# Expert selection of a two-block model: gates of all heads normalised in one go, and a triangle of 112 candidate sums in place of a 16 x 16 square

## The chip, the cores and the metric

One core of a Trainium2 chip runs the whole program once. The metric is the device time of one execution in microseconds (us). The kernel before takes 2967.11 us (median of three runs, 2965.75 to 2971.43).

The engines are named as the profile names them: PE is TensorE (PEld its weight loads), DVE is VectorE, ACT is ScalarE, POOL is GpSimd and SP is SyncE. Each engine works through its own instructions in the order in which the program issues them; between engines they wait on semaphores.

## The reference, cut to what matters

Two transformer blocks over 256 tokens of width 2048. The change is in the second block's mixture of experts (PEER): for each token and each of eight heads, two lists of 128 key scores are cut to their sixteen largest, all sums of one key of either list are formed, the sixteen largest sums choose sixteen experts, and a softmax over these sixteen sums gives the gates.

```python
v1, i1 = lax.top_k(s1, PEER_TOPK)
v2, i2 = lax.top_k(s2, PEER_TOPK)
cand = (v1[..., :, None] + v2[..., None, :]).reshape(B, S, PEER_HEADS, PEER_TOPK * PEER_TOPK)
vs, ci = lax.top_k(cand, PEER_TOPK)
e1 = jnp.take_along_axis(i1, ci // PEER_TOPK, axis=-1)
e2 = jnp.take_along_axis(i2, ci % PEER_TOPK, axis=-1)
eidx = e1 * PEER_NKEYS + e2
gates = jax.nn.softmax(vs, axis=-1).astype(xn.dtype)
...
act = jax.nn.gelu(jnp.einsum('tkd,td->tk', expert_u[ib], xb))
return jnp.einsum('tk,tkd->td', act * gb, expert_v[ib])
```

So every token has 8 x 16 = 128 experts, and each of these needs a row of `expert_u` (2048 floats) for its activation and a row of `expert_v` for its output.

## The kernel before

The 256 tokens stand as two tiles of 128 partitions (`tt` is 0 or 1). The part in question runs like this.

**Scores.** `project1` makes the 16 query blocks on PE from weight chunks that SP loads (`raw<-w_pq`). `pq_done` copies a block from PSUM on ACT, `score` multiplies it by the keys on PE and writes the scaled scores to `sc` on ACT. Head h has its scores when two such blocks are through.

**Choice.** `topk(0)` works through heads 0, 2, 4, 6 and `topk(1)` through 1, 3, 5, 7; both are Python generators in lanes that are stepped in turn after every second matmul of the projection (`beside`). So the order on each engine is fixed when the program is written. For one head:

- `top16` on the four lists of 128 scores, on DVE: the eight largest, their positions, removal of these eight, the next eight, their positions;
- on POOL the positions are cast (L1599) and two squares of 16 x 16 sums are formed (L1601);
- `top16` on DVE on the two lists of 256 sums; `vs` are the values and `ci` the positions;
- the decode on POOL (L1606 to L1611): the position is cast to float, divided by 16 and rounded by adding and subtracting a large constant, which gives the row; 16 times the row is taken off, which gives the column. L1612 negates the largest sum;
- a comparison on DVE (L1616) of these numbers with 0 to 15, four multiplications on POOL by the keys' positions (L1618), a sum on DVE (L1624), and three instructions on POOL that form the expert's number and put it in `idx` (L1626 to L1628);
- for the gates an exponential with its sum on ACT (L1620, two instructions), a reciprocal on DVE (L1625) and a scaling on POOL (L1633).

**Rows.** As soon as a head has its `idx`, `u_rows` lets POOL issue gathers (L1663): one gather brings one row of `expert_u` for each of 128 tokens, into one of ten seats (four for the second tile of tokens). DVE multiplies each by the tokens (L1703, 256 times) and sums it, which frees the seat for the gather ten further on. While the heads are still being chosen, these multiplications stand between the steps of `topk` on DVE.

**After the eighth head** `slots_` copies the gates (L1640) and transposes the experts' numbers (L1644 to L1647). When 128 multiplications of a tile of tokens are done, `weights` applies the activation and the gates. `spots` then builds matrices for the dense half of `expert_v`, which PE multiplies at L1900, and the other half is gathered and summed by `v_rows` (L1840).

Of the kernel before, what the change touches and what calls it, by code (L numbers as in the profile page):

```python
# [10 lines left out]
U32 = mybir.dt.uint32  # L11
AF = mybir.ActivationFunctionType
OP = mybir.AluOpType
AX = mybir.AxisListType

T = 256
# [209 lines left out]
def program(tc, A, out, stage=99, dbg=None):  # L226
# [26 lines left out]
    V, S, G, PE, SP = nc.vector, nc.scalar, nc.gpsimd, nc.tensor, nc.sync  # L253
# [333 lines left out]
    p = bank(bgN, "pn")  # L587
# [47 lines left out]
    bias = cM(8, T)  # L635
# [4 lines left out]
    wide = cM(2, 128)  # L640
# [14 lines left out]
    oh, past = cW(512, p=32), cW(512, p=8)  # L655
# [872 lines left out]
    xs = dram.tile([128, 16, T], F32, name="xs")  # L1528
    SP.dma_start(xs, x)
    cK = Carve("cK")  # L1530
    subk, qring, eg, ek, kk = cK(8, 2, 128), cK(4, T), cK(2, 128), cK(8, 2, 2, 16), cK(2, 128)
    G.dma_start(subk.rearrange("p h s n -> p (h s n)"), A["subk"])
    sc = slab("sc").rearrange("p (t h s n) -> p t h s n", t=2, h=8, s=2)
    cT = Carve("cT")
    e1T, e2T, wT = sq[:, 0], sq[:, 1], acc_sq
    gate_ = rb.rearrange("p (t s) -> p t s", t=2)
    wv = sm.rearrange("p a b -> p (a b)").rearrange("p (t s) -> p t s", t=2)
# [47 lines left out]

    def topk(first):

        cand, oh = cT(2, 16, 16), cT(2, 2, 16, 16)
        vv, ii, iif = cT(2, 2, 16), cT(2, 2, 16).bitcast(U32), cT(2, 2, 16)
        vs, ci, cf, c1, gs = cT(2, 16), cT(2, 16).bitcast(U32), cT(2, 16), cT(2, 2, 16), cT(2, 4)  # L1590
        xf = cT(2, 16)
        flat = lambda v: v.rearrange("p t s n -> p (t s n)")
        for h in range(first, 8, 2):
            while flags.get(("sc", h), 0) < 2:
                yield
            hs = slice(h * 16, h * 16 + 16)
            both = [(tt, s) for tt in range(2) for s in range(2)]
            yield from top16([(sc[:, tt, h, s], vv[:, tt, s], ii[:, tt, s]) for tt, s in both])
            G.tensor_copy(iif, ii)  # L1599
            for tt in range(2):  # L1600
                G.tensor_add(cand[:, tt], vv[:, tt, 0][:, :, None].to_broadcast([128, 16, 16]),  # L1601
                             vv[:, tt, 1][:, None, :].to_broadcast([128, 16, 16]))
            yield
            yield from top16([(cand[:, tt].rearrange("p a b -> p (a b)"), vs[:, tt], ci[:, tt]) for tt in range(2)])

            G.tensor_copy(cf, ci)  # L1606
            G.tensor_scalar(c1[:, :, 0], cf, 1.0 / 16, -7.5 / 16, op0=OP.mult, op1=OP.add)
            G.tensor_scalar(c1[:, :, 0], c1[:, :, 0], 1.5 * 2.0 ** 23, None, op0=OP.add)
            G.tensor_scalar(c1[:, :, 0], c1[:, :, 0], 1.5 * 2.0 ** 23, None, op0=OP.subtract)
            G.tensor_scalar(c1[:, :, 1], c1[:, :, 0], -16.0, None, op0=OP.mult)  # L1610
            G.tensor_add(c1[:, :, 1], c1[:, :, 1], cf)  # L1611
            G.tensor_scalar(gs[:, :, 0], vs[:, :, 0], -1.0, None, op0=OP.mult)  # L1612
            io = iota[:, 0:16][:, None, :].to_broadcast([128, 64, 16])
            yield
            sel = oh.rearrange("p t s a b -> p (t s a) b")
            V.tensor_tensor(sel, flat(c1)[:, :, None].to_broadcast([128, 64, 16]), io, op=OP.is_equal)  # L1616
            for tt, s in both:
                G.tensor_mul(oh[:, tt, s], oh[:, tt, s], iif[:, tt, s][:, None, :].to_broadcast([128, 16, 16]))  # L1618
            for tt in range(2):
                S.activation(eg[:, tt, hs], vs[:, tt], AF.Exp, bias=gs[:, tt, 0:1], accum_out=gs[:, tt, 1:2])  # L1620
            yield
            yield
            yield
            V.tensor_reduce(flat(ek[:, h]), sel, axis=AX.X, op=OP.add)  # L1624
            V.reciprocal(gs[:, :, 2], gs[:, :, 1])  # L1625
            G.tensor_scalar(xf, ek[:, h, :, 0], 128.0, None, op0=OP.mult)  # L1626
            G.tensor_add(xf, xf, ek[:, h, :, 1])
            G.tensor_copy(idx[:, :, hs], xf)  # L1628
            flags[("idx", h)] = True
            yield  # L1630
            for tt in range(2):
                g = eg[:, tt, hs]
                G.tensor_scalar(g, g, gs[:, tt, 2:3], None, op0=OP.mult)  # L1633
            flags["heads"] = flags.get("heads", 0) + 1

    def slots_():

        while flags.get("heads", 0) < 8:
            yield
        G.tensor_copy(gate_, eg)  # L1640
        for tt in range(2):
            p = bank(bgA, "pa")
            for k in range(2):
                G.tensor_copy(kk[:, k].rearrange("p (h n) -> p h n", h=8), ek[:, :, tt, k])  # L1644
                PE.transpose(p[:, k * 128:k * 128 + 128], kk[:, k], ident)
            for k, d in enumerate((e1T, e2T)):
                S.copy(d[:, tt * 128:tt * 128 + 128], p[:, k * 128:k * 128 + 128])  # L1647
            yield
        flags["topk"] = True
# [228 lines left out]
    for k in range(128):  # L1878
# [14 lines left out]
        for j in range(8):  # L1893
            w, _ = next_block()
# [60 lines left out]
```

## Time and profile before

| what | value |
|---|---|
| median of three runs | 2967.11 us |
| the profiled execution's own time | 2963.08 us |
| its span, first to last instruction | 2961.3 us |
| busy: PE, DVE, ACT, POOL | 2311.8, 1999.7, 1191.2, 900.9 us |
| mean granted clock of TensorE | 0.878 of full speed |
| groups of instructions at L1703: count, busy | 256, 580.3 us |

The shares over the whole span say little here, since the program runs in stages with different limits. The choice of experts lies between about 1519 and 1702 us of the span, the stream of `expert_u` rows between 1542 and about 2270 us, the dense half of `expert_v` and the second stream of rows behind that. To read the profile, one goes to that stretch: what the chain of work that ended last runs through there, and whether the DMA engines are full.

### The profile page before, as it was taken

What the parts mean: (1) busy time and instruction counts of PE and PEld (TensorE: products, weight loads), DVE (VectorE), ACT (ScalarE), POOL (GpSimd) and SP (SyncE); (2) the same over time, 40 slices, a digit from 0 to 9 for tenths busy, and PEclk for the clock granted to TensorE, in tenths of its full rate; (3) what the DMA queues carried; (4) which work ended last, traced back from release to release, by engine and by line L of the source; (5) the groups of instructions that cost most, each with busy time, mean ns of one, the idle gap of its engine ahead of it and who ended that gap; (6) DMA issues with size and microseconds to landing.
All of it is one profiled execution on the core that took longest, in us unless ns stands there. A gap on an engine that the chain in (4) does not pass through costs nothing.

```text
span 2961.3 us, 39499 instructions
## 1 busy us (share of the span) xinstructions
PE 2311.8 (78%) x14635; PEld 2106.1 (71%) x14635; DVE 1999.7 (68%) x2615; ACT 1191.2 (40%) x2560; POOL 900.9 (30%) x1262
## 2 busy tenths in 40 slices
PE   8999999999999999999997200022222999999799
PEld 8887898888889999998986200011122988888689
DVE  5455666555556565656537999988998866666655
ACT  4355555444444454445411000058880444400043
POOL 3202215111111000331135543333334555555420
PEclk9999999999999999999998655555555799999999
DMA  6444455655655555543557799999997799999945
GB/s 221 153 128 122 134 158 180 196 188 187 197 187 190 185 180 184 172 151 109 182 201 279 291 407 422 422 397 408 415 415 317 265 403 404 395 401 409 366 148 166
DMA packets 174675, 765.11 MB, mean 258 GB/s; under 512 B 19585, under 2 KB 22049, under 8 KB 141201
## 3 DMA queue, kind: packets, MB, share of 16 engines
q1 hardware_dynamic: 99216, 353.83, 36.0%
q0 software_dynamic: 75264, 408.75, 34.5%
q8 instruction: 115, 1.88, 0.3%
q14 instruction: 80, 0.65, 0.1%
HBM read 757.77 MB, written 4.21 MB: 257 GB/s over the span
## 4 chain that ended last, share of the span: by engine, by line
PE 59%; DMA 12%; DVE 10%; issue 9%; POOL 8%; ACT 1%; another core or an unknown queue 0%; SPq 0%; POOLq 0%; DVEq 0%; ACTq 0%
PE acc L411 11%; PE acc L1900 7%; PE acc L386 6%; PE acc L388 6%; PE acc L387 6%; DMA rows<-w_vs,idx 6%; PE acc L412 6%; POOL rows L1663 5%; DMA rows<-w_u,idx 5%; DVE rows L1703 5%; PE acc L485 3%; PE acc L483 3%; PE acc L484 3%; PE sp L1794 1%; DMA raw<-w_vd 1%
## 5 line engine op out<-in xcount | busy, mean ns | idle before, releaser
L350 DVE TENSOR_TENSOR wlo<-raw,whi 128x1024 fp32r<-128x1024 f32 (+1 forms) x501 | 613.5, 1233 | 415.1 <-ACT whi L349 408.3
L349 ACT CAST whi<-raw 128x1024 fp32r<-128x1024 f32 (+1 forms) x501 | 519.7, 1042 | 380.2 <-PE acc L387 130.9
L1703 DVE SCALAR_TENSOR_TENSOR rows<-rows,yt 128x2048 f32<-128x2048 f32 x256 | 580.3, 2285 | 42.9 <-DMA rows<-w_u,idx 38.6
L1900 PE MATMUL acc<-G,raw 128*128 128x256 f32 x2048 | 457.3, 385 | 12.4 <-DMA raw<-w_vd 11.1
L1900 PEld LDWEIGHTS acc<-G,raw 128*128 128x128 f32 x2048 | 391.8, 193 | 71.7 <-DMA raw<-w_vd 17.0
L1840 DVE SCALAR_TENSOR_TENSOR sacc<-rows,sm,sacc 128x1024 f32<-128x1024 f32 x254 | 327.3, 1289 | 143.8 <-DMA rows<-w_vs,idx 127.4
L1663 POOL DMA_INDIRECT rows<-w_u,idx x256 | 244.2, 954 | 380.0 <-DVE rows L1703 274.8
L1663 POOL DMA_INDIRECT rows<-w_vs,idx x256 | 248.8, 972 | 149.6 <-DVE sacc L1840 81.7
L411 PE MATMUL acc<-xl,whi 128*128 128x512 f32 x704 | 248.2, 391 | 0.0
L411 PE MATMUL acc<-xh,whi 128*128 128x512 f32 x704 | 248.1, 391 | 0.0
L1762 PE MATMUL sp<-P,Q 128*128 128x128 f32 x256 | 60.2, 430 | 213.9 <-ACT P L1758 213.9
L1762 PEld LDWEIGHTS sp<-P,Q 128*128 128x128 f32 x256 | 55.8, 330 | 218.6 <-ACT P L1758 218.6
L564 POOL TENSOR_TENSOR acc_sq<-acc_sq,sq 128x256 f32<-128x256 f32 x63 | 57.0, 904 | 504.6 <-ACT sq L563 502.7
L485 PE MATMUL acc<-ring,wlo 128*128 128x256 f32 x704 | 199.3, 283 | 0.1
L483 PE MATMUL acc<-ring,whi 128*128 128x256 f32 x704 | 199.3, 283 | 0.1
L484 PE MATMUL acc<-ring,whi 128*128 128x256 f32 x704 | 199.2, 283 | 0.0
L412 PE MATMUL acc<-xh,wlo 128*128 128x256 f32 x704 | 197.2, 280 | 0.0
L412 PE MATMUL acc<-xl,wlo 128*128 128x256 f32 x704 | 197.1, 280 | 0.0
L1659 PE MATMUL yt<-keep,xg 128*128 128x128 f32 x32 | 5.6, 350 | 237.6 <-DVE rows L1703 237.1
L1191 POOL TENSOR_TENSOR hT<-cF 128x256 f32<-128x256 f32 x44 | 70.8, 1609 | 372.7 <-ACT whi L349 342.8
L1659 PEld LDWEIGHTS yt<-keep,xg 128*128 128x128 f32 x32 | 5.0, 184 | 238.1 <-DVE rows L1703 237.3
L386 PE MATMUL acc<-xh,whi 128*128 128x256 f32 x520 | 150.6, 290 | 3.2 <-ACT whi L349 1.8
(486 smaller groups left out, 5692.7 us busy)
## 6 DMA issues: line engine op xcount, KB each, us to landing
raw<-w_gu SPq DMA_DIRECT2D x176, 512.0 KB
raw<-w_vd SPq DMA_DIRECT2D x128, 512.0 KB
raw<-w_down SPq DMA_DIRECT2D x88, 512.0 KB
raw<-w_out SPq DMA_DIRECT2D x32, 512.0 KB
raw<-w_pq SPq DMA_DIRECT2D x32, 512.0 KB
raw<-w_pg SPq DMA_DIRECT2D x32, 512.0 KB
raw<-w_b SPq DMA_DIRECT2D x24, 512.0 KB
raw<-w_lat SPq DMA_DIRECT2D x18, 512.0 KB
```

Of the source, the lines that this page charges most:

```text
L349: S.copy(hi[j][:, a:b], raw[j][:, a:b])
L350: V.tensor_sub(lo[j][:, a:b], raw[j][:, a:b], hi[j][:, a:b].bitcast(F32))
L386: PE.matmul(ps, wh, xh, start=start, stop=False, **k)
L411: PE.matmul(ps, wh, xh.both(k), start=k == 0, stop=False, skip_group_check=True)
L412: PE.matmul(ps[:, :T], wl, xh[:, k], start=False, stop=k == kb - 1, skip_group_check=True)
L483: PE.matmul(o, wh, ah, start=(k == 0 and j % 2 == 0), stop=False, skip_group_check=True)
L484: PE.matmul(o, wh, al, start=False, stop=False, skip_group_check=True)
L485: PE.matmul(o, wl, ah, start=False, stop=(k == nk - 1), skip_group_check=True)
L1663: G.indirect_dma_start(dst, None, src, bass.IndirectOffsetOnAxis(ap=idx[:, tt, s:s + 1], axis=0))
L1703: V.scalar_tensor_tensor(r, r, 1.0, accT, op0=OP.mult, op1=OP.mult, accum_out=wv[:, tt, s:s + 1])
L1840: V.scalar_tensor_tensor(sacc, r, w, sacc, op0=OP.mult, op1=OP.add)
L1900: PE.matmul(o, w, gs_[k // 16][:, k % 16], start=(k == 0 and j % 2 == 0), stop=k == 127, skip_group_check=True)
```

## The change

The two squares of 256 sums become two lists of 112: rows 0 to 3 of the square with all 16 columns (64 sums) and rows 4 to 15 with columns 0 to 3 (48 sums). The position in such a list no longer is 16 times the row plus the column, so the decode has more steps. The sixteen largest sums of every head go to one tile `vsa`, and the exponential, its sum, the reciprocal and the scaling are made once for all heads, in `slots_`.

```diff
-        cand, oh = cT(2, 16, 16), cT(2, 2, 16, 16)
+        cand, oh = cT(2, 112), cT(2, 2, 16, 16)
...
             for tt in range(2):
-                G.tensor_add(cand[:, tt], vv[:, tt, 0][:, :, None].to_broadcast([128, 16, 16]),
-                             vv[:, tt, 1][:, None, :].to_broadcast([128, 16, 16]))
-            yield
-            yield from top16([(cand[:, tt].rearrange("p a b -> p (a b)"), vs[:, tt], ci[:, tt]) for tt in range(2)])
+                for a, na, nb, at in ((0, 4, 16, 0), (4, 12, 4, 64)):
+                    G.tensor_add(cand[:, tt, at:at + na * nb].rearrange("p (a b) -> p a b", a=na),
+                                 vv[:, tt, 0, a:a + na][:, :, None].to_broadcast([128, na, nb]),
+                                 vv[:, tt, 1, 0:nb][:, None, :].to_broadcast([128, na, nb]))
+            yield
+            vs = vsa[:, h]
+            yield from top16([(cand[:, tt], vs[:, tt], ci[:, tt]) for tt in range(2)])
 
             G.tensor_copy(cf, ci)
-            G.tensor_scalar(c1[:, :, 0], cf, 1.0 / 16, -7.5 / 16, op0=OP.mult, op1=OP.add)
-            G.tensor_scalar(c1[:, :, 0], c1[:, :, 0], 1.5 * 2.0 ** 23, None, op0=OP.add)
-            G.tensor_scalar(c1[:, :, 0], c1[:, :, 0], 1.5 * 2.0 ** 23, None, op0=OP.subtract)
-            G.tensor_scalar(c1[:, :, 1], c1[:, :, 0], -16.0, None, op0=OP.mult)
-            G.tensor_add(c1[:, :, 1], c1[:, :, 1], cf)
-            G.tensor_scalar(gs[:, :, 0], vs[:, :, 0], -1.0, None, op0=OP.mult)
+            i_, j_, r_ = c1[:, :, 0], c1[:, :, 1], 1.5 * 2.0 ** 23
+            G.tensor_scalar(i_, cf, 1.0 / 16, -7.5 / 16, op0=OP.mult, op1=OP.add)
+            G.tensor_scalar(i_, i_, r_, None, op0=OP.add)
+            G.tensor_scalar(i_, i_, r_, None, op0=OP.subtract)
+            G.tensor_scalar(j_, cf, 0.25, -12.375, op0=OP.mult, op1=OP.add)
+            G.tensor_scalar(j_, j_, r_, None, op0=OP.add)
+            G.tensor_scalar(j_, j_, r_, None, op0=OP.subtract)
+            G.tensor_scalar(far, cf, 1.0 / 112, -7.5 / 112, op0=OP.mult, op1=OP.add)
+            G.tensor_scalar(far, far, r_, None, op0=OP.add)
+            G.tensor_scalar(far, far, r_, None, op0=OP.subtract)
+            G.tensor_sub(j_, j_, i_)
+            G.tensor_mul(j_, j_, far)
+            G.tensor_add(i_, i_, j_)
+            G.tensor_scalar(xf, i_, 12.0, -48.0, op0=OP.mult, op1=OP.add)
+            G.tensor_mul(xf, xf, far)
+            G.tensor_scalar(j_, i_, -16.0, None, op0=OP.mult)
+            G.tensor_add(j_, j_, cf)
+            G.tensor_add(j_, j_, xf)
...
-            for tt in range(2):
-                S.activation(eg[:, tt, hs], vs[:, tt], AF.Exp, bias=gs[:, tt, 0:1], accum_out=gs[:, tt, 1:2])
...
-            V.reciprocal(gs[:, :, 2], gs[:, :, 1])
...
-            for tt in range(2):
-                g = eg[:, tt, hs]
-                G.tensor_scalar(g, g, gs[:, tt, 2:3], None, op0=OP.mult)
...
     def slots_():
 
         while flags.get("heads", 0) < 8:
             yield
-        G.tensor_copy(gate_, eg)
+        for _ in range(2):
+            yield
+        wide = [128, 16, 16]
+        gs = kk.rearrange("p k n -> p (k n)")[:, 0:16]
+        G.tensor_copy(gs, ga[:, :, 0])
+        G.tensor_tensor(ga, ga, gs[:, :, None].to_broadcast(wide), op=OP.subtract)
+        yield
+        S.activation(ga, ga, AF.Exp)
+        for _ in range(2):
+            yield
+        V.tensor_reduce(gs, ga, axis=AX.X, op=OP.add)
+        V.reciprocal(gs, gs)
+        G.tensor_mul(gate_.rearrange("p t (h n) -> p h t n", h=8), vsa, gs.rearrange("p (h t) -> p h t", t=2)[:, :, :, None]
+                     .to_broadcast([128, 8, 2, 16]))
```

The order of the instructions on PE and SP is the same in both kernels, and on DVE and ACT it differs by the instructions named above alone. On POOL, the decode of one head stands like this before (`cT` is the slab that holds all small tiles of `topk`; a wait on Pool_49 is a wait for an earlier instruction of POOL itself):

```order
L1606 CAST cT<-cT 128x32 [waits DVE_49]
L1607 TENSOR_SCALAR cT<-cT 128x2x16 [waits Pool_49]
L1608 TENSOR_SCALAR cT<-cT 128x2x16 [waits Pool_49]
L1609 TENSOR_SCALAR cT<-cT 128x2x16 [waits Pool_49]
L1610 TENSOR_SCALAR cT<-cT 128x2x16 [waits Pool_49]
L1611 TENSOR_TENSOR cT<-cT 128x2x16 [waits Pool_49]
L1612 TENSOR_SCALAR cT<-cT 128x2
L1618 TENSOR_TENSOR cT<-cT 128x256 [waits DVE_49]
```

In the changed kernel the same place begins like this on POOL:

```order
L1612 CAST cT<-cT 128x32 [waits DVE_49]
L1614 TENSOR_SCALAR cT<-cT 128x2x16 [waits Pool_49]
L1615 TENSOR_SCALAR cT<-cT 128x2x16 [waits Pool_49]
L1616 TENSOR_SCALAR cT<-cT 128x2x16 [waits Pool_49]
L1617 TENSOR_SCALAR cT<-cT 128x2x16
L1618 TENSOR_SCALAR cT<-cT 128x2x16 [waits Pool_49]
L1619 TENSOR_SCALAR cT<-cT 128x2x16 [waits Pool_49]
L1620 TENSOR_SCALAR cT<-cT 128x32
L1621 TENSOR_SCALAR cT<-cT 128x32 [waits Pool_49]
L1622 TENSOR_SCALAR cT<-cT 128x32 [waits Pool_49]
L1623 TENSOR_TENSOR cT<-cT 128x2x16
L1624 TENSOR_TENSOR cT<-cT 128x2x16 [waits Pool_49]
```

Six more follow (L1625 to L1630, all but L1628 with a wait on Pool_49) before the multiplications, which are L1636 there. The comparison on DVE (L1616 before, L1634 in the changed kernel) waited for the sixth of these instructions and now waits for the eighteenth.

Behind the eighth head POOL's order was this (`rows` are the seats, `cK` holds the gates and the experts' numbers, `rb` takes the gates):

```order
L1628 CAST idx<-cT 128x2x16 [waits Pool_49]
L1633 TENSOR_SCALAR cK<-cK,cT 128x16 [waits DVE_49]
L1633 TENSOR_SCALAR cK<-cK,cT 128x16 [waits Activation_49]
L1640 COPY rb<-cK 128x256 [waits Pool_49]
L1644 COPY cK<-cK 128x128 x2
L1663 DMA rows_15108<-w_u,idx 128x2048 [waits DMASW6_49,DVE_49]
L1644 COPY cK<-cK 128x128 [waits PE_49] x2
L1663 DMA rows_15109<-w_u,idx 128x2048 [waits DMASW7_49,DVE_49]
```

In the changed kernel POOL has there:

```order
L1643 CAST idx<-cT 128x2x16 [waits Pool_49]
L1688 DMA rows_15108<-w_u,idx 128x2048 [waits DMASW6_49,DVE_49]
L1688 DMA rows_15109<-w_u,idx 128x2048 [waits DMASW7_49,DVE_49]
L1656 COPY cK<-cT 128x16
L1657 TENSOR_TENSOR cT<-cT,cK 128x256 [waits Pool_49]
L1688 DMA rows_15109<-w_u,idx 128x2048 [waits DMASW0_49,DVE_49]
L1688 DMA rows_15110<-w_u,idx 128x2048 [waits DMASW1_49,DVE_49]
L1688 DMA rows_15110<-w_u,idx 128x2048 [waits DMASW2_49,DVE_49]
L1664 TENSOR_TENSOR rb<-cT,cK 128x8x2x16 [waits DVE_49,Activation_49]
L1669 COPY cK<-cK 128x128 [waits Pool_49]
L1669 COPY cK<-cK 128x128
L1688 DMA rows_15106<-w_u,idx 128x2048 [waits DMASW3_49]
```

Five gathers now stand ahead of the gates' last step (L1664), which waits for DVE's reciprocal; the sixth gather stands behind it.

## Rows read from the trace of the kernel before

**Rows 1.** Busy time of each engine in stretches: start:end, length, then each engine.
```profile
core 0: us, PE busy (x) PEld busy (x) DVE busy (x) ACT busy (x) POOL busy (x), PEclk, DMA share, GB/s
1600.00:1690.00 90.00, 37.48 (x155) 31.52 (x153) 82.29 (x219) 6.72 (x27) 43.58 (x80) 0.71 0.81 308
1690.00:1702.00 12.00, 0.00 (x0) 0.00 (x0) 10.47 (x23) 0.69 (x4) 8.21 (x14) 0.50 0.54 190
1702.00:1790.00 88.00, 1.42 (x4) 0.73 (x4) 88.00 (x81) 2.15 (x5) 39.53 (x49) 0.50 0.99 407
1790.00:1930.00 140.00, 0.00 (x0) 0.00 (x0) 130.82 (x117) 0.00 (x0) 52.45 (x56) 0.50 1.01 422
1930.00:2250.00 320.00, 64.11 (x273) 59.26 (x273) 287.66 (x251) 238.81 (x770) 115.97 (x125) 0.55 1.00 410
```
**Rows 2.** Chain that ended last, head 2: start us, us, what.
```profile
1568.72 0.81 DVE cT L1583 x2
1569.59 0.22 POOL cT L1606
1569.89 0.23 POOL cT L1607
1570.20 0.31 POOL cT L1608
...
1570.96 0.30 POOL cT L1610
1571.34 0.26 POOL cT L1611
1571.62 1.24 DVE cT L1616
1572.93 2.79 POOL cT L1618 x4
1575.74 1.22 DVE cK L1624
```
**Rows 3.** The same chain at heads 0, 1 and 5.
```profile
1540.67 0.09 DVE cT L1625
...
1543.41 0.65 POOL cK L1633 x2
...
1550.67 0.95 POOL rows L1663
1551.62 0.23 POOL cT L1606
...
1644.23 0.20 POOL cT L1612
```
**Rows 4.** Groups of 1490 to 1790 us: busy us, mean ns | idle before.
```profile
L1601 POOL TENSOR_TENSOR cT<-cT 128x256 f32<-128x256 f32 x16 | 9.6, 618 | 0.0
...
L1580 DVE MAX8 cT<-sc 128x8 f32<-128x128 f32 x32 | 6.9, 277 | 0.0
...
L1580 DVE MAX8 cT<-cT 128x8 f32<-128x256 f32 x16 | 5.9, 413 | 0.0
```
**Rows 5.** Waits, 1490 to 1800 us: total us, times, longest us.
```profile
ACT cK L1620 <- POOL cT L1612: 109.9, 8, 21.0
...
DVE cT L1572 <- ACT sc L1555: 18.4, 2, 14.9
...
DVE cT L1616 <- POOL cT L1611: 13.5, 5, 4.8
```
**Rows 6.** Instructions of DVE and POOL around the end of the eighth head, in time.
```profile
1644.27 1.22 DVE L1616 TENSOR_TENSOR cT<-cT,keep 128x1024 f32<-128x1024 f32 x1
...
1700.81 1.22 DVE L1624 TENSOR_REDUCE cK<-cT 128x64 f32<-128x1024 f32 x1 [1.52 <-POOL cT L1618]
...
1702.02 2.27 DVE L1703 SCALAR_TENSOR_TENSOR rows<-rows,yt 128x2048 f32<-128x2048 f32 x1
...
1704.21 2.28 DVE L1703 SCALAR_TENSOR_TENSOR rows<-rows,yt 128x2048 f32<-128x2048 f32 x1
```

More of the change, by code (lines that the diff above doesn't have):

```diff
@@ L1530, in program @@
     cK = Carve("cK")
-    subk, qring, eg, ek, kk = cK(8, 2, 128), cK(4, T), cK(2, 128), cK(8, 2, 2, 16), cK(2, 128)
+    subk, qring, ek, kk = cK(8, 2, 128), cK(4, T), cK(8, 2, 2, 16), cK(2, 128)
     G.dma_start(subk.rearrange("p h s n -> p (h s n)"), A["subk"])
@@ L1534, in program @@
     cT = Carve("cT")
+    vsa = cT(8, 2, 16)
+    ga = vsa.rearrange("p h t n -> p (h t) n")
     e1T, e2T, wT = sq[:, 0], sq[:, 1], acc_sq
@@ L1586, in topk @@
     def topk(first):
-        cand, oh = cT(2, 16, 16), cT(2, 2, 16, 16)
+        cand, oh = cT(2, 112), cT(2, 2, 16, 16)
         vv, ii, iif = cT(2, 2, 16), cT(2, 2, 16).bitcast(U32), cT(2, 2, 16)
-        vs, ci, cf, c1, gs = cT(2, 16), cT(2, 16).bitcast(U32), cT(2, 16), cT(2, 2, 16), cT(2, 4)
-        xf = cT(2, 16)
+        ci, cf, c1 = cT(2, 16).bitcast(U32), cT(2, 16), cT(2, 2, 16)
+        xf, far = cT(2, 16), cT(2, 16)
         flat = lambda v: v.rearrange("p t s n -> p (t s n)")
```

## The prediction

> **What bounds the kernel now.** The shares over the whole span do not help, so I read three things for the stretch of the change. First the busy time by stretch [rows 1]. From 1702 us on, the DMA engines are full (share 0.99 to 1.01, 405 to 422 GB/s) until the rows of `expert_u` have come, at about 2250. Ahead of that they are not: 0.81 in 1600 to 1690, and 0.54 in the last 12 us before the eighth head is done. Ahead of 1702 DVE is what is busy (82.29 of 90 us), with holes. So the row stream becomes a fixed amount of transfer that starts at full rate only when the choice of experts ends, and the end of the choice (the sum over head 7's comparison, L1624 at 1700.81 [rows 6]) is what carries the rest of the program with it.
>
> Second, the chain of waits in that stretch [rows 2]. For head 2 it leaves DVE after the last position search (L1583), goes through every small POOL instruction of the decode (1569.59 to 1571.60, 2.01 us), back to DVE for the comparison (1571.62), to POOL for the multiplications (2.79 us) and to DVE for the sum. The decode is on the path, instruction by instruction. Third, the waits [rows 5]: DVE stood 13.5 us for the decode in five of eight heads, while scores made it wait 18.4 us in only two places, both ahead of the first head. ACT waited 109.9 us for the decode, but nobody on the path waited for ACT.
>
> **The change part by part.**
>
> **Shorter lists on DVE.** Per head ten instructions (four MAX, four index searches, two replacements) run over 112 columns and not 256. A MAX takes 277 ns over 128 columns and 413 over 256 [rows 4], so 136 ns go per 128 columns, which I take for the searches and replacements too: 0.136 x 144 / 128 = 0.153 us per instruction. Nine of ten count: between the two first MAX DVE waits for POOL's sums, which come no sooner. That is 9 x 0.153 = 1.38 us per head. In head 1 it gives nothing: POOL is busy with five gathers until 1551.62 and starts the decode right behind them, later than DVE is ready [rows 3]. So 7 x 1.38 = 9.6 us go.
>
> **Sums on POOL.** Two adds of 256 columns at 618 ns [rows 4] become four of 64 or 48. A POOL instruction of two inputs takes 0.25 us for 32 columns (L1611 [rows 2]), so a column costs (0.618 - 0.25) / 224 = 0.0016 us, and the new ones 0.30 and 0.28: 0.58 for a list against 0.62. Nothing.
>
> **The decode.** Before, the comparison waited for six instructions, 2.01 us; it now waits for eighteen. Their spacing comes from [rows 2]. The cast is followed after 0.30 us. A scaling with two operations (L1607) is followed by an instruction that needs its result after 0.31 us. One with a single operation (L1608) is followed by such an instruction after 0.38 us, of which it is busy 0.30; where the next one needs nothing of it I take these 0.30. An instruction with two inputs is busy 0.25; with the same gap of 0.08 it is followed after 0.33. Of the eighteen: one cast (0.30), four scalings with two operations (L1614, L1617, L1620, L1626: 1.24), four single ones followed by a dependent one (L1615, L1618, L1621, L1628: 1.52), three followed by an independent one (L1616, L1619, L1622: 0.90), four of two inputs followed by a dependent one (1.32), one not (0.25), and the last (0.26). The sum is 5.79 us, 3.78 more than before, and 8 x 3.78 = 30.2 us over eight heads. Is any of it hidden? Where nothing stands between search and comparison on DVE (heads 0 to 3) it is bare. In heads 5 to 7 one row multiplication stands between (2.2 us), but the old decode filled that cover already: in head 5 the last instruction of the decode ends at 1644.23, where L1612 starts [rows 3], and the comparison starts at 1644.27 [rows 6]. So all of it is on the path.
>
> Bounds from both sides: if each of the twelve added instructions took the shortest spacing that these rows show for any, 0.22 us, the decode grows by 2.6 us (21.1 in all); if the longest, 0.38, by 4.6 (36.5). I take 3.78, since the order tells which depend on the one before, and since the rows are of the same shape.
>
> The Trainium skill speaks against this term: its page "GPSIMD Engine Reference", section "Instruction dispatch", puts the cost of a POOL instruction's dispatch at tens of cycles, and its section "Elementwise — side-by-side cycle accounting" the elements at about 2.6 cycles each. By that page a 32-column instruction is, as my estimate at the 1.2 GHz that "Trainium Kernel Development and Optimization" gives, about 0.1 us, twelve are 1.2 us, and the change would come out near no change. The trace does not agree: the same shape holds POOL 0.22 to 0.31 us.
>
> **What leaves the path with the gates.** The reciprocal leaves DVE: 0.09 us per head [rows 3], 0.7 in all. The two scalings L1633 stood ahead of the next head's sums in head 1 only (0.65 us [rows 3]); elsewhere POOL waited for DVE there. L1612 (0.20 [rows 3]) stood between decode and multiplications where a gather follows it, heads 1, 5 and 7: 0.6. ACT loses sixteen exponentials, so PE's scores and the last weight chunks come sooner; I put that at nothing, because DVE never waited for scores after the first head [rows 5], and no transfer leaves the full stretch by it (DMA is idle for 46% of the 12 us before 1702 [rows 1], so those chunks are through).
>
> **The gates behind the last head.** POOL's last step of the gates waits for DVE's reciprocal, which stands behind six row multiplications, and the sixth gather is queued behind it. That gather waits for the sixth of these multiplications anyway, so what is added is the sum over 256 columns and the reciprocal on DVE and three POOL instructions, some 1.5 to 2 us. The next gathers catch up, since a gather holds POOL for 0.95 us [rows 3] and seats come free every 2.2 us (L1703 starts at 1702.02 and 1704.21 [rows 6]). By then five gathers have been issued faster than they land, 2.2 against 1.05 MB / 422 GB/s = 2.49 us [rows 1], so the DMA engines have work meanwhile. I put it at nothing, 2 us if that cover fails. The gates are needed only when 128 rows are done, after 1930.
>
> **Sum.** 30.2 - 9.6 - 0.7 - 0.65 - 0.6 = 18.7 us later at the end of the eighth head. Behind it the stream is transfer at a full rate and everything else hangs on it, so the end moves by as much: the profiled execution's 2963.08 becomes 2981.8. The median of the runs stands 4.0 above that execution, so I predict 2967.1 + 18.7 = 2985.8 us. With the two bounds of the decode the sum is 9.6 and 25.0: 2977 to 2992.
>
> **The rivals.**
>
> *Faster: a long train of small POOL instructions costs only its columns.* If the fixed part of each vanished behind the one before, an added instruction would cost 32 x 0.0016 = 0.05 us, twelve 0.6, eight heads 4.9, and 4.9 - 11.5 = -6.6 us gives 2960.5. It decides from 11.5 / 96 = 0.12 us per added instruction down. For it: the dependent ones are spaced by a wait, and five of the added have none. Against it: the old train of six takes 2.01 us, 0.33 each. By the page named above the price lies near this point. Chance 0.06.
>
> *The same: the stream of rows swallows it.* The rows' transfers are a fixed amount, and were gathers queued deep enough at 1702, a later end of the choice would only eat into the queue. It takes 18.7 / 2.49 = 7.5 gathers in the queue. For it: the DMA engines are full for all of the next 550 us. Against it: 0.54 in the last 12 us. The time would be about 2967. Chance 0.10.
>
> *More: the spacing is longer, and the gates hold the stream up.* All twelve at 0.38 us and above, the wait for the reciprocal not covered: 25.0 + 2 and more, 2994 to 2997. Chance 0.09.
>
> **How the numbers follow.** The forecast has 0.75, and it is slower by more than 0.2% (5.9 us, about what a measurement of this kernel tells from no change) over all of 2977 to 2992. With the last rival slower has 0.84, the same 0.10, faster 0.06. Leaving out the first two rivals leaves 0.16 outside; the range runs from a little under the lower bound of the decode to the last rival: 2974 to 2995.
>
> **What would show it.** In the changed kernel's trace the train from the cast L1612 to L1630 should take about 5.8 us per head, and DVE's idle time ahead of its comparison should rise from 13.5 to about 40 us. MAX over 112 columns should take about 0.26 us. The sum of the eighth head should stand at about 1719.5 us instead of 1700.81, and the distance from there to the end of the span should be unchanged within 2 us. The first would be wrong if the train takes under 3.5 us, the last if the DMA engines' share is near 1 already ahead of the eighth head. ACT's long waits should be gone without effect on the end.

## The result and the profile after

The changed kernel takes 2989.1 us (median of 6 runs, 2978.05 to 2993.9) against 2966.43 us for the kernel before on the same chip (6 runs, 2959.45 to 2971.43). The ratio is 1.0067, with an interval of 1.0046 to 1.0088: 0.0067 x 2966.43 = 19.9 us slower, between 13.6 and 26.1; the two medians differ by 22.7. Forecast were 18.7 us and 2985.8.

The profiled execution of the changed kernel is the lowest of its six runs (2978.05 us, span 2976.3, against 2963.08 and 2961.3 before), so its span moved by 15.0 us only. Where these belong is told below; first the stretch that the prediction spoke of. These are the waits of the changed kernel from 1490 to 1820 us (total us, times, longest us), where [rows 5] had 13.5 us for the comparison and 109.9 us for ACT:

```profile
ACT cT L1659 <- POOL cT L1657: 115.1, 1, 115.1
...
DVE cT L1634 <- POOL cT L1630: 46.3, 8, 10.0
...
DVE cT L1574 <- ACT sc L1557: 18.4, 2, 14.9
DVE cK L1640 <- POOL cT L1636: 13.9, 7, 3.7
...
DVE cT L1574 <- POOL cT L1605: 7.9, 12, 2.4
```

DVE waits for the decode (now L1612 to L1630) in all eight heads and not in five, 46.3 us in place of 13.5. Its other waits are what they were: 18.4 for scores, 13.9 for the multiplications (14.0 before). ACT's eight waits became one, the exponential of all gates at L1659.

The chain that ended last, at head 2, goes through the decode as in [rows 2], with three times as many links (start us, us, what; "issue" is time in which the engine waited for nothing that the profile shows):

```profile
1574.71 0.22 POOL cT L1612
1574.93 0.08 issue
1575.01 0.23 POOL cT L1614
...
1575.31 0.31 POOL cT L1615
...
1575.69 0.29 POOL cT L1616
...
1576.05 0.23 POOL cT L1617
...
1577.76 0.29 POOL cT L1622
1578.05 0.22 POOL cT L1623
...
1580.35 0.26 POOL cT L1630
1580.63 1.24 DVE cT L1634
```

From the cast at 1574.71 to the end of L1630 at 1580.61 are 5.9 us, where [rows 2] had 2.01 for six instructions. Nearly every link is 0.22 to 0.31 us of work and 0.06 to 0.08 us of gap. Four of the added instructions need nothing of the one in front (L1617, L1620, L1623 and L1628). Of these only L1623 has no gap; L1617 starts 0.36 us behind L1616, of which 0.29 are work, as if it had to wait. What the shorter lists and the other sums cost is in the groups from 1490 to 1810 us (busy us, mean ns of one | idle before):

```profile
L1605 POOL TENSOR_TENSOR cT<-cT 128x64 f32<-128x64 f32 x16 | 4.7, 291 | 0.0
...
L1605 POOL TENSOR_TENSOR cT<-cT 128x48 f32<-128x48 f32 x16 | 4.2, 262 | 0.0
L1582 DVE MAX8 cT<-cT 128x8 f32<-128x112 f32 x16 | 3.6, 264 | 0.0
```

A MAX over 112 columns takes 264 ns against 413 over 256 [rows 4], and the two adds of a list 0.291 + 0.262 = 0.55 us against 0.62. The end of the eighth head stands here, in time, and as the last line the last of the 256 row multiplications:

```profile
1716.90 1.22 DVE L1634 TENSOR_TENSOR cT<-cT,keep 128x1024 f32<-128x1024 f32 x1 [3.80 <-POOL cT L1630]
1721.84 1.22 DVE L1640 TENSOR_REDUCE cK<-cT 128x64 f32<-128x1024 f32 x1 [1.51 <-POOL cT L1636]
...
2287.58 2.29 DVE L1728 SCALAR_TENSOR_TENSOR rows<-rows,yt 128x2048 f32<-128x2048 f32 x1 [0.15 <-DMA rows<-w_u,idx]
```

The eighth head's sum was at 1700.81 [rows 6] and is at 1721.84. DVE now stands 3.80 us for the last decode. And the stretches (columns as in [rows 1]):

```profile
core 0: us, PE busy (x) PEld busy (x) DVE busy (x) ACT busy (x) POOL busy (x), PEclk, DMA share, GB/s
1600.00:1700.00 100.00, 13.38 (x67) 11.44 (x65) 78.53 (x206) 2.62 (x8) 52.74 (x118) 0.59 0.63 224
1710.00:1720.00 10.00, 0.00 (x0) 0.00 (x0) 6.20 (x11) 0.00 (x0) 7.60 (x22) 0.50 0.37 116
1720.00:1810.00 90.00, 1.42 (x4) 0.73 (x4) 88.45 (x84) 2.57 (x6) 42.07 (x52) 0.50 0.99 398
```

Ahead of the eighth head's end the DMA engines have less to do than before: a share of 0.63 and then 0.37, where [rows 1] has 0.81 and 0.54. From 1720 on they are full (0.99), as they were from 1702 on before.

To compare kernels I split each profiled execution at three instructions: the first cast of positions on POOL (L1599, after L1601), the eighth head's sum on DVE, and the last multiplication of a row of `expert_u`. The *choice* lies between the first two, the *rows* between the second and the third, the *tail* from there to the end of the span.

| us | choice begins | choice | rows | tail | span | DVE's wait before the comparison |
|---|---|---|---|---|---|---|
| before | 1527.7 | 173.1 | 567.1 | 693.4 | 2961.3 | 13.5 |
| after | 1529.1 | 192.7 | 565.8 | 688.7 | 2976.3 | 46.3 |

The choice is 19.6 us longer, the rows 1.3 shorter. The tail, which holds nothing that the change touches, is 4.7 us shorter in this one execution. In the fourteen executions profiled for this study it lies between 687.5 and 694.7 us in no order that goes with any edit. The stretch ahead of the choice varies too: the choice begins between 1527.7 and 1540.0 us, in code that no edit touches. The tail is most of why the span moved by 15.0 us where the medians differ by 22.7; and these two stretches are why the experiments below are read by choice and rows first, and by their timed ratio second.

### The profile page after: what moved, and what is told of

The parts are those of the page before. It is cut to its first block, busy times and chain, and to the rows that moved or that the text cites. A ratio compares the mean times of both kernels' runs of the same rounds, so it can differ in the third digit from the quotient of the medians.

```text
span 2976.3 us, 39542 instructions
## 1 busy us (share of the span) xinstructions
PE 2296.7 (77%) x14635; PEld 2095.6 (70%) x14635; DVE 1989.5 (67%) x2609; ACT 1187.0 (40%) x2529; POOL 919.5 (31%) x1352
## 4 chain that ended last, share of the span: by engine, by line
PE 58%; DMA 13%; issue 9%; DVE 9%; POOL 9%; ACT 1%; POOLq 0%; SPq 0%; DVEq 0%; ACTq 0%
PE acc L411 11%; PE acc L1925 7%; DMA rows<-w_vs,idx 6%; PE acc L386 6%; PE acc L388 6%; PE acc L387 6%; PE acc L412 6%; DMA rows<-w_u,idx 5%; POOL rows L1688 5%; DVE rows L1728 5%; PE acc L485 3%; PE acc L483 3%; PE acc L484 3%; PE sp L1819 1%; PE acc L456 1%
```

## The experiments

Three kernels first, to part the change into its pieces; then three that load or move the decode; then five that put other work over it, one of them run twice. That one, the kernel before with the row lane moved, took 480.0 and 482.1 us for its rows in its two profiled executions, so differences of some 2 us in the rows say nothing. Ratios are against the kernel before on the same chip, with a 95% interval.

**The gates alone.** The kernel before, with the gates of all heads made behind the last one; 256 sums and the decode of six instructions stay.

```
-            for tt in range(2):
-                S.activation(eg[:, tt, hs], vs[:, tt], AF.Exp, bias=gs[:, tt, 0:1], accum_out=gs[:, tt, 1:2])
...
+        G.tensor_tensor(ga, ga, gs[:, :, None].to_broadcast(wide), op=OP.subtract)
+        yield
+        S.activation(ga, ga, AF.Exp)
```

> The kernel before with the gates of all heads made in one go behind the eighth head; squares of 256 sums and the old decode stay. Theory (the decode train on POOL is the whole loss): the eighth head ends about 2.0 us sooner against the start of the choice (reciprocals 0.7, L1633 0.65, L1612 0.6), so about 2965 us, no change that a time can show; ACT's waits for the decode are gone without effect. Rival (the gates' last step holds up the gathers behind it): 2 to 5 us slower, with the DMA engines idle shortly after the eighth head.

Measured: 2964.19 us against 2970.22, 0.9982 [0.9964, 0.9999]. Choice 171.8 us (1.3 shorter), rows 569.7, DVE's wait before the comparison 13.4. ACT no longer waits for any head's decode, and that shows nowhere on the path. The gates alone give 1.3 us in the choice; the rows behind it are 2.6 us longer, which is about their spread. In the time it is 0.18%, between 0.01 and 0.36, and the choice accounts for only a quarter of these 5 us.

**The lists alone.** The kernel before, with 112 sums and their decode; the gates stay with each head.

```
-        cand, oh = cT(2, 16, 16), cT(2, 2, 16, 16)
+        cand, oh = cT(2, 112), cT(2, 2, 16, 16)
...
+            G.tensor_scalar(far, cf, 1.0 / 112, -7.5 / 112, op0=OP.mult, op1=OP.add)
```

> The kernel before with the 112 sums and their longer decode, gates per head as before. Theory: 30.2 us for the decode less 9.6 for the shorter lists, 20.6 us later at the eighth head's end and about 2987 us. Rival (the loss comes from the gates): no slower than before, 2957 to 2967 us.

Measured: 2986.88 us, 1.0059 [1.0039, 1.0079]. Choice 193.8 us (20.7 longer), rows 567.7. The whole loss is in the lists and their decode. This is the group of the comparison in this kernel, 1490 to 1820 us:

```profile
L1631 DVE TENSOR_TENSOR cT<-cT,keep 128x1024 f32<-128x1024 f32 x8 | 9.8, 1225 | 46.3 <-POOL cT L1626 46.3
```

The same 46.3 us of waiting as in the changed kernel, with the gates as they were.

**The change without its decode.** The changed kernel with the six instructions of before; positions are read as if all 256 sums were there, so it picks other experts and its rows are others, at the same cost each.

```
-            G.tensor_scalar(j_, cf, 0.25, -12.375, op0=OP.mult, op1=OP.add)
...
-            G.tensor_add(j_, j_, xf)
+            G.tensor_scalar(c1[:, :, 1], c1[:, :, 0], -16.0, None, op0=OP.mult)
+            G.tensor_add(c1[:, :, 1], c1[:, :, 1], cf)
```

> The changed kernel with 112 sums and gates in one go, but the decode of the kernel before (six instructions ahead of the comparison and not eighteen). It leaves out the right decode of positions in the list of 112, so it picks other experts. Theory: what is left is the gain of the shorter lists and of the gates, 9.6 + 2.0 = 11.6 us sooner, about 2955 us. Rival (the decode is no loss, something else in the change is): as slow as the changed kernel, about 2986 us.

Measured: 2958.12 us, 0.9959 [0.9941, 0.9978]. Choice 161.3 us, 11.8 shorter than before; the wait before the comparison is 15.2. So what the change saves is there, and the sum put it at 9.6 + 0.7 + 0.65 + 0.6 = 11.55 us. From this kernel to the changed one the choice grows by 192.7 - 161.3 = 31.4 us, for which the sum had 30.2.

**Twelve more in the old decode.** The kernel before, nothing else changed:

```
             G.tensor_add(c1[:, :, 1], c1[:, :, 1], cf)
+            for _ in range(12):
+                G.tensor_scalar(c1[:, :, 1], c1[:, :, 1], 1.0, None, op0=OP.mult)
```

> The kernel before with twelve more instructions of 128x32 in a dependent train at the end of the decode, each multiplying by 1. Theory (each added POOL instruction stands on the path at its spacing): 12 x 0.38 = 4.6 us per head, 36.5 over eight, about 3003 us. Rival (the stream of rows swallows a later end of the choice): about 2967 us although the eighth head ends 36 us later. Rival (small POOL instructions in a train cost their columns alone, 0.05 us): 2972 us.

Measured: 3009.42 us, 1.0110 [1.0073, 1.0147]. Choice 208.5 us, 35.4 longer. The added group and the comparison's, 1490 to 1820 us:

```profile
L1613 POOL TENSOR_SCALAR cT<-cT 128x32 f32<-128x32 f32 x96 | 27.6, 288 | 8.0
...
L1618 DVE TENSOR_TENSOR cT<-cT,keep 128x1024 f32<-128x1024 f32 x8 | 9.8, 1225 | 48.8 <-POOL cT L1613 48.8
```

Twelve single scalings that hang on one another are busy 288 ns each and cost 35.4 / 96 = 0.37 us each in the choice, the 0.38 that the prediction read in [rows 2]. The price of an instruction in this place is not the price of its columns.

**The same twelve in another place.** Is it POOL's load, or the place? Twelve such instructions behind the cast of the finished indices, where no later step of the same head's choice waits for their result (on POOL the next gathers stand behind them):

```
             G.tensor_copy(idx[:, :, hs], xf)
+            for _ in range(12):
+                G.tensor_scalar(xf, xf, 1.0, None, op0=OP.mult)
```

> The kernel before with the same twelve added instructions per head on POOL as in the run longer12, but behind the cast to idx and not ahead of the comparison. Theory (what counts is that DVE's comparison waits for the train, not that POOL has more to do): only where POOL has no idle time ahead of the next head's sums do they move the end of the choice, by 4.6 us in head 1, 3.8 in head 2, 1.4 in head 3 and nothing behind; 9.8 us later, about 2980 us beside 2970 for the kernel before. Rival (the load of POOL counts, wherever it stands): as in longer12, 35 us later.

Measured: 2981.43 us against 2969.72, 1.0043 [1.0026, 1.0060]. Choice 182.0 us, 8.9 longer, a quarter of 35.4. Two groups of this kernel, 1490 to 1820 us:

```profile
L1616 DVE TENSOR_TENSOR cT<-cT,keep 128x1024 f32<-128x1024 f32 x8 | 9.8, 1223 | 13.5 <-POOL cT L1611 13.5
...
L1572 DVE MAX8 cT<-cT 128x8 f32<-128x256 f32 x16 | 6.6, 424 | 17.9 <-POOL cT L1601 17.0
```

The comparison waits 13.5 us, as before; the added wait is that of the MAX for POOL's sums, 17.0 for 8.1 before. The rows are longer too, 573.7 us for 567.1, which I had not expected. Part of that is to be seen on POOL behind the eighth head:

```profile
1713.94 4.37 POOL L1630 TENSOR_SCALAR cT<-cT 128x32 f32<-128x32 f32 x12
...
1719.99 1.02 POOL L1665 DMA_INDIRECT rows<-w_u,idx  x1 [0.16 <-issue]
```

The eighth head's own twelve stand between its indices (cast at 1713.64) and the next gather, 4.37 us at a moment when the DMA engines are not full (a share of 0.38 from 1714 to 1720). The other 2 us are within the spread of the rows.

**The same decode on DVE.** The changed kernel, with its eighteen instructions issued by `V` in place of `G`, one for one.

```
-            G.tensor_copy(cf, ci)
+            V.tensor_copy(cf, ci)
...
-            G.tensor_add(j_, j_, xf)
+            V.tensor_add(j_, j_, xf)
```

> The changed kernel with its eighteen decode instructions moved from POOL to DVE, one for one. Theory (the handover to POOL and its spacing of 0.32 us are the loss): at an estimated 0.2 us each, between the 0.09 of the reciprocal's piece in the chain and the 0.25 that the last reciprocal is busy, the train is 3.6 us; heads 0 to 4 are 2.3 us shorter each, heads 5 to 7 are not, since a row multiplication now stands behind the train and not beside it. The choice is 11 us shorter than in the changed kernel, some 8 us longer than before. Rival (DVE's spacing is no shorter than POOL's): as long as in the changed kernel or longer.

Measured: 2970.58 us, 1.0003 [0.9983, 1.0022]. Choice 173.0 us, as before the change, where I had expected 181 or 182. The train of head 5, first and last row, and what follows it:

```profile
1666.68 0.32 DVE L1612 CAST cT<-cT 128x32 f32<-128x32 uint32 x1
...
1670.02 0.19 DVE L1630 TENSOR_TENSOR cT<-cT 128x32 f32<-128x32 f32 x1
1670.13 2.28 DVE L1728 SCALAR_TENSOR_TENSOR rows<-rows,yt 128x2048 f32<-128x2048 f32 x1
```

From 1666.68 to 1670.13 are 3.45 us, 0.19 per instruction where POOL took 0.33, near the 0.2 that I had put. Counted from one head's sum to the next, the choice is shorter than in the changed kernel by 2.5 us in heads 0 (from the choice's beginning), 2 and 3, 3.1 in head 4, 0.6 to 1.1 in heads 5 to 7, and 6.5 in head 1. In head 1 the train on POOL starts only behind five gathers, and DVE stands 10.0 us for it; on DVE it does not queue behind them. That head and the last three are what I had missed. So the move takes away two things, POOL's spacing and the place in POOL's queue, and that eight heads of 5.9 - 3.45 come to the same 19.6 us is chance. The arithmetic as such is not the loss: on DVE the same eighteen steps cost what the shorter lists save. The rows are 570.8 us, 3.7 longer than before, which stays open.

**Cover for the decode.** The choice runs beside a lane that multiplies rows, and in the code as it stands that lane starts at head 4. Three edits, in the changed kernel and in the kernel before alike, put two row multiplications between the last search and the comparison of a head:

```
             io = iota[:, 0:16][:, None, :].to_broadcast([128, 64, 16])
             yield
+            yield
...
-        while heads() < 4:
+        while heads() < 1:
...
-            for _ in range(2 if heads() < 8 else 0):
+            for _ in range(1 if heads() < 8 else 0):
```

In the changed kernel:

> The changed kernel with row multiplications put where DVE waits: they start behind the first head and not the fourth, one in two steps of the lanes and not one in three, and the comparison stands one step later, so that two of them (4.4 us) lie between the last search and the comparison in heads 1 to 7. Theory (the loss is bare waiting on DVE, and the stream is transfer that starts late): 60 rows and not 25 are done by the end of the choice, DVE's idle time ahead of the comparison falls from 46 to about 15 us, and the last row comes 25 to 40 us sooner than in the changed kernel, 2950 to 2965 us. Rival (DVE's time is full either way and the rows only move): as slow as the changed kernel.

In the kernel before:

> The kernel before with the same three edits to the lanes as in cover_after. Theory: with cover for the decode, the long train of the changed kernel costs little and its shorter lists are what is left, so this is as fast as cover_after or up to 12 us slower. Rival (the long train costs as much as without cover): cover_before is 18 us or more faster than cover_after.

Measured: 2957.58 us, 0.9950 [0.9927, 0.9973], with the change, and 2935.66 us, 0.9898 [0.9849, 0.9946], without it. Both gain from the lane, since some 60 rows are done by the end of the choice (the rows behind it take 480 to 486 us, not 567). But I had expected the change to cost nothing under cover, and it costs as much as without: 22 us. The choice holds 60 rows in both kernels (25 without the lane), so I compare the last row's multiplication, counted from the choice's beginning: 731.8 us with the change, 709.0 without (740.2 in the kernel before without the lane). The groups of the comparison in both, 1490 to 1820 us, the change first:

```profile
L1635 DVE TENSOR_TENSOR cT<-cT,keep 128x1024 f32<-128x1024 f32 x8 | 9.8, 1226 | 20.7 <-POOL cT L1630 20.7
```

```profile
L1617 DVE TENSOR_TENSOR cT<-cT,keep 128x1024 f32<-128x1024 f32 x8 | 9.8, 1222 | 1.3 <-POOL cT L1611 1.3
```

Two multiplications are 4.4 us and the train is 5.9: 1.9 us stay bare in each of heads 3 to 7, and 2.6 to 5.2 in heads 0 to 2. The old decode, 2.0 us, is covered but for 1.3 us in head 0. Two more kernels ask whether that is all.

**More cover.** The changed kernel with the same lane and three more `yield` in place of one, so that three multiplications stand there.

> The changed kernel with the lanes of cover_after, but the comparison two steps later still, so that three row multiplications (6.6 us) and not two (4.4) lie between the last search and the comparison in heads 2 to 7. Theory (cover_after missed because two multiplications leave 1.5 us of the 5.9 us train bare in each head): DVE's idle time ahead of the comparison falls from 20.7 us to under 10, and the run comes some 10 to 14 us sooner than cover_after, about 2945 us beside 2970 for the kernel before. Rival (what cover_after lost lies elsewhere, in the rows' transfers): no sooner than cover_after, 2957.

Measured: 2951.39 us against 2973.3, 0.9941 [0.9913, 0.9968]. DVE's waits, 1490 to 1820 us, here and then in the kernel before with the lane:

```profile
DVE cK L1643 <- POOL cT L1639: 16.6, 6, 2.8
...
DVE rows L1731 <- DMA rows<-w_u,idx: 13.3, 6, 8.1
...
DVE cT L1574 <- POOL cT L1605: 7.5, 8, 2.5
...
DVE cT L1637 <- POOL cT L1630: 4.0, 2, 2.4
```

```profile
DVE cK L1625 <- POOL cT L1619: 6.0, 7, 1.8
...
DVE rows L1704 <- DMA rows<-w_u,idx: 5.6, 1, 5.6
...
DVE cT L1572 <- POOL cT L1601: 2.7, 2, 1.7
...
DVE cT L1617 <- POOL cT L1611: 1.3, 1, 1.3
```

The comparison's wait is gone as expected, 4.0 us; the last row comes 9.5 us sooner than with two (722.3 us after the choice's beginning), and that is still 13 us later than without the change. The time went into other waits: for the multiplications 16.6 for 6.0, for the rows 13.3 for 5.6, for the sums 7.5 for 2.7. All four rows together are 41.4 us against 15.6. Of these 25.8 us the shorter lists give back 8 x 1.38 = 11.0 by the forecast, which leaves 14.8 for the 13.3 seen. The train, then, is hidden from its own head and pays elsewhere.

For the longest of these waits, that for the multiplications, the rows show how. This is POOL in head 3, here (the comparison stands at 1642.50 to 1643.72) and in the kernel before with the lane (1630.88 to 1632.10):

```profile
1642.74 1.87 POOL L1691 DMA_INDIRECT rows<-w_u,idx  x1 [0.46 <-DVE rows L1731]
...
1644.92 0.95 POOL L1691 DMA_INDIRECT rows<-w_u,idx  x1 [0.30 <-DMA rows<-w_u,idx]
1645.89 2.76 POOL L1639 TENSOR_TENSOR cT<-cT 128x256 f32<-128x256 f32 x4
```

```profile
1629.09 1.02 POOL L1664 DMA_INDIRECT rows<-w_u,idx  x1 [0.26 <-DVE rows L1704]
1632.19 2.78 POOL L1619 TENSOR_TENSOR cT<-cT 128x256 f32<-128x256 f32 x4 [2.08 <-DVE cT L1617]
```

Behind the short decode the gather is out before the comparison starts, and the multiplications follow the comparison at once. Behind the long train the gather falls beside the comparison, where it takes 1.87 us, another follows it, and only then come the multiplications. From comparison to sum are 6.2 us in heads 2 to 7 here, 4.9 with two multiplications as cover and the long train, 4.1 in the kernel before with the lane. That the waits for the rows and the sums grow because POOL is fuller is argued, from these rows and from the twelve behind the indices, which cost 8.9 us there.

**Gates under cover.** The kernel with the lists alone, with the lane of two multiplications: ACT's exponentials per head hold the scores' last work back again.

> The kernel before with the 112 sums, their long decode and the lanes of cover_after, gates per head as before, so that ACT again waits for each decode and holds back PE and the last weight chunks. Theory (the train is the loss here too): DVE stands about 20 us ahead of the comparison as in cover_after, and the time is the same, 2955 to 2962. Rival (in cover_after the weight chunks, no longer held back, take transfer time from the rows while the DMA engines are full): DVE waits less for rows than the 8.4 us of cover_after and the run is 5 us or more sooner.

Measured: 2949.24 us, 0.9922 [0.9897, 0.9947]. Last row 722.5 us after the choice's beginning, 9.3 sooner than with the gates in one go: 2.3 in the choice and 7.0 behind it. DVE's wait before the comparison is the same, 20.2 us, and its wait for rows too, 7.9 for 8.4. So in these traces the gates in one go cost something under the lane, where without it they cost nothing; but the intervals of the two ratios overlap ([0.9897, 0.9947] and [0.9927, 0.9973]), so the time does not settle it, and by what mechanism the 7 us come behind the choice is open.

**A shorter list with a shorter decode.** If the price is the train, a list that is a little longer but decodes in fewer steps should win. The kernel before with the lane, and 136 sums: the sixteen partners of each of the eight largest first keys, and one partner of each of the other eight. Its decode has ten instructions on POOL.

```
-        cand, oh = cT(2, 16, 16), cT(2, 2, 16, 16)
+        cand, oh = cT(2, 136), cT(2, 2, 16, 16)
...
+                for a, na, nb, at in ((0, 8, 16, 0), (8, 8, 1, 128)):
...
+            G.tensor_scalar(far, cf, 127.5, None, op0=OP.is_ge)
+            G.tensor_scalar(j_, i_, -16.0, None, op0=OP.mult)
+            G.tensor_add(j_, j_, cf)
+            G.tensor_mul(far, far, j_)
+            G.tensor_add(i_, i_, far)
+            G.tensor_sub(j_, j_, far)
```

> The lanes of cover_before with lists of 136 sums (rows 0 to 7 with all 16 columns, rows 8 to 15 with column 0), whose decode takes ten instructions on POOL and not eighteen, gates per head. Theory: the train is about 3.4 us and lies under the 4.4 us of two row multiplications, so the shorter lists (120 columns less, ten instructions, 0.127 us each, 10 us over eight heads) are gained on DVE; as the DMA engines were idle for only some 12 us of the choice in cover_before, 5 to 10 us sooner than cover_before. Rival (in cover_before the rows' transfers already set the pace): as fast as cover_before.

> The kernel of cover_before again, beside cover_136 on the same chip: 2931 to 2940 us.

Measured on one chip: 2929.63 us, 0.9855 [0.9833, 0.9878], and for the kernel before with the lane, run once more beside it, 2933.15 us, 0.9861 [0.9840, 0.9881]. The group of its comparison, 1490 to 1820 us:

```profile
L1624 DVE TENSOR_TENSOR cT<-cT,keep 128x1024 f32<-128x1024 f32 x8 | 9.8, 1225 | 2.6 <-POOL cT L1618 2.6
```

Ten instructions fit under two multiplications (2.6 us of waiting in all), and the gather behind them starts 0.3 us ahead of the comparison in heads 2 to 7 and takes 1.02 us; from comparison to sum are 4.1 us, as with the old decode. The choice is 6.8 us shorter and the last row 6.3 sooner. The median is 3.5 us lower, but the intervals overlap: nearly all of the 1.5% over the kernel before comes from the lane, and what the shorter list adds is in the trace and not settled in the time.

## Why the prediction was right

The mechanism, its place and its size were as forecast. Point by point:

- **The decode.** Forecast 5.79 us per head, measured 5.9. The spacing by kind holds: two operations 0.30, one operation 0.38 with a dependent one behind it, two inputs 0.33. What does not hold is that an instruction with an independent one behind it has no gap: these four were put at 0.30 three times and 0.25, and take 0.36, 0.35, 0.29 and 0.32, together 0.17 us more, which is why 5.9 lies above the forecast. Against the same kernel without its long decode the choice is 31.4 us longer (forecast 30.2). The range's ends, 0.22 and 0.38 per added instruction, held it: 31.4 / 96 = 0.33. The faster rival needed under 0.12. Every head pays: counted from sum to sum, seven heads are 2.2 to 2.7 us longer than before and head 1 is 3.0, where the shorter lists give nothing, as forecast.
- **The page that spoke against it.** The trace shows 0.22 to 0.31 us of busy time per 32-column instruction in the changed kernel too, and 0.37 per instruction in the twelve added to the old decode. The Trainium skill, page "GPSIMD Engine Reference", sections "Instruction dispatch" and "Elementwise — side-by-side cycle accounting", gave an estimate of about 0.1 us and near no change; the run with twelve more (1.0110) speaks against it for this shape.
- **Shorter lists and what left with the gates.** Forecast 11.55 us together, measured 11.8, and that this is so near is in part luck, since two terms miss and cancel. The gates' part was put at 2.0 us and measured at 1.3 by themselves. What came to nothing are the 0.6 us for L1612: in heads 1, 5 and 7 the sum comes 4.9 to 5.0 us behind the comparison in the kernel before, in the changed one and in the one with the gates alone, since the gather in between ends 0.9 us behind the comparison in all three (more of this in the last section). That leaves 10.5 us for the lists, put at 9.6. The MAX over 112 takes 264 ns, forecast 260; but POOL's sums of a head, put at no gain, take 0.98 us in place of 1.19, and DVE waits for them.
- **DVE's idle time** before the comparison was to be about 40 us and is 46.3. That number was loose by its own terms: 13.5 + 30.2 are 43.7. The wait grows by 3.8 to 4.2 us in seven heads and by 5.2 in head 1, where the shorter lists bring DVE to the comparison sooner but the train still starts behind the gathers.
- **The end of the eighth head.** Forecast 1719.5, measured 1721.84, of which 1.4 us are an execution that began its choice later (1529.1 for 1527.7). The choice by itself: +19.6 for a forecast of +18.7.
- **Carried to the end one to one.** The rows behind the choice take 565.8 us for 567.1: nothing is given back. The rival in which the stream swallows the delay had a queue of 7.5 gathers as its condition; a DMA share of 0.37 just ahead of the end speaks against such a queue, and the rows, no more than 1.3 us shorter, show that next to nothing of the delay was swallowed. The forecast that the distance to the end of the span stays within 2 us missed in that one execution (6 us shorter, 4.7 of it in the tail), which is within the spread of the tail over executions, and the timed ratio gives 19.9.
- **The gates behind the last head** were put at nothing. POOL's last step waits 1.8 us for the reciprocal. The rows of DVE and POOL from there, in time:

```profile
1736.22 0.42 DVE L1662 TENSOR_REDUCE cK<-cT 128x16 f32<-128x256 f32 x1
1736.67 0.25 DVE L1663 RECIPROCAL cK<-cK 128x16 f32<-128x16 f32 x1
```

```profile
1737.08 0.62 POOL L1664 TENSOR_TENSOR rb<-cT,cK 128x256 f32<-128x256 f32 x1 [1.75 <-DVE cK L1663]
...
1738.44 1.01 POOL L1688 DMA_INDIRECT rows<-w_u,idx  x1 [0.15 <-issue]
...
1741.56 0.95 POOL L1688 DMA_INDIRECT rows<-w_u,idx  x1 [0.44 <-DVE rows L1728]
```

  Counted from the end of the multiplication that frees the seat, two gathers go out 1.9 and 0.8 us later than those ahead of them, the one at 1741.56 waits for its buffer again, and the DMA share of 1720 to 1810 is 0.99: covered, as put.
- **ACT's long waits** left without effect on the end, as forecast: the gates alone give 0.9982, less than the 0.2% that the prediction took as a bound.

What I would have got wrong, had it been asked, is the remedy: that a decode under row multiplications is free. It is not, as the kernels with the lane show.

## What to carry to other kernels

Count instructions, not elements, where small steps stand in a row between two engines: here an instruction of 32 columns costs 0.33 us in a train on POOL, most of it whether the next one depends on it or not, and 0.19 on DVE; an edit that saves columns on one engine has to be paid for in links on the other (the shorter lists gave 1.3 us per head, twelve more links took 3.9). Price the place of a step before its size: the same twelve instructions cost 35.4 us ahead of the comparison and 8.9 behind the indices. And before shortening a path, look at what could run beside it: starting the row lane sooner gave 1.0 to 1.4%, more than any form of the list did.

## What the runs showed that was not expected

A gather that POOL issues is busy for 0.95 to 1.02 us in the rows above, but longer where it falls beside the comparison on DVE (1716.90 to 1718.12 in the changed kernel):

```profile
1717.32 1.70 POOL L1688 DMA_INDIRECT rows<-w_u,idx  x1 [0.46 <-issue]
```

It is 1.70 us, 0.75 more, and stands ahead of the multiplications of the last head. The kernel before has the same there, beside its comparison at 1695.86 to 1697.08, and the changed kernel has a longer one in head 1, beside the comparison at 1560.40 to 1561.63:

```profile
1696.28 1.71 POOL L1663 DMA_INDIRECT rows<-w_u,idx  x1 [0.26 <-issue]
```

```profile
1560.52 2.01 POOL L1688 DMA_INDIRECT rows<-w_u,idx  x1 [0.15 <-issue]
```

All three end 0.9 us behind the end of the comparison, wherever they started, and 0.9 is about what a gather takes by itself. So do all 45 gathers in the fourteen traces that start while a comparison runs: they end 0.81 to 0.91 us behind its end. Beside the row multiplications on DVE a gather takes its 0.95 us. The gather looks held up until the comparison is over; what holds it was not tried. It is why the removal of L1612 gave nothing, and why under the lane it matters on which side of the comparison the train lets the gather go.

On DVE the eighteen instructions of the decode follow each other every 0.19 us on average, faster than the 0.22 us of busy time that the shortest of them has on POOL. There it does matter what needs what: in head 5 the four that need nothing of the one in front follow after 0.09 to 0.11 us, what stands behind any other after 0.20 to 0.23, and behind the cast after 0.36.
